# Where the split weights and the activations of a decoder layer lie in a partition

## The chip, the cores and the metric

The kernel runs on one core of a Trainium2 chip. The metric is device time of one execution in microseconds (us); lower is better. Engines are TensorE (PE, with its weight loads PEld), VectorE (DVE), ScalarE (ACT), GpSimd (POOL) and SyncE (SP).

## The reference

One inference step of one layer (D_MODEL 2048) on 256 prompt tokens and 8 x 4 sample tokens, in fp32. Cut to what matters:

```python
def hybrid_layer(x, conv_a_buf, gdn_buf, S0, w_in, ...):
    proj = x @ w_in                                   # 2048 x 11280
    gB, gC, h, q, k, v, z, b_logit, a_logit, m_a, m_b = jnp.split(proj, split_points, axis=-1)
    conv_out, new_conv_a = causal_depthwise_conv(gC * h, conv_a_buf, conv_a_w)
    y_a = (gB * conv_out) @ w_a_out
    qkv, new_gdn_buf = causal_depthwise_conv(jnp.concatenate([q, k, v], -1), gdn_buf, gdn_conv_w)
    ...                                               # gated delta rule in chunks of 64, norm, silu(z)
    y_b = o.reshape(Bsz, L, D_GDN).astype(x.dtype) @ w_b_out
    merged = jax.nn.sigmoid(m_a) * y_a + jax.nn.sigmoid(m_b) * y_b
    x = layer_norm(ALPHA * x + merged @ w_o, ln1_g, ln1_b)
    hid = jnp.square(jax.nn.relu(x @ w_up))           # 2048 x 8192
    x = layer_norm(ALPHA * x + hid @ w_down, ln2_g, ln2_b)
    return x, new_conv_a, new_gdn_buf, S.astype(S0.dtype)
```

## The kernel before

All tokens (256 + 32 = 288 columns, `NT`) stand in the free dimension; features lie on the 128 partitions, in k tiles of 128 (`KT` = 16 for 2048 features). A fp32 product is made of three fp32r matmuls: the weights are split into `hi` (rounded) and `lo` (the rest), the activations likewise, and hi x high, hi x low and lo x high are summed in PSUM.

Weights pass in blocks of 512 x 256 (four k tiles of 256 output columns; blocks of the first group and those of paired groups have `kb` = 2 k tiles of 512 columns). The list `blocks` is the order of the work, written out by hand: input projection (kqv, conv, z), gates merged with `w_a_out` and `w_b_out`, `w_o`, then four times an up-projection of 2048 columns and the down-projection that uses it. The main loop runs over the blocks. For block i it lets ACT make `his[i + 3]` from `raw[i + 3]` (`split_hi`, L187), DVE make `los[i + 3]` (`split_lo`, recorded at L142, the helper `tt`), and then issues the 24 matmuls of block i (`matmuls`, L219 for hi, L221 for lo): for each k tile, hi half 0 with the high and the low activations, hi half 1 with both, then lo half 0 and lo half 1 with the high ones. Each matmul loads its own 128 x 128 weights. The evacuation of a finished group is hung on the next blocks. The first six blocks are split just ahead of their use, with parts of a block at a time (`split_first`, and `step` in the split functions). Loads go through SP's queue, seven blocks ahead.

Buffers before: `raw`, `hi` and `lo` are tiles of 4096 bytes in a partition, four of each, in the pool `wp`; a block's k tiles follow each other at 1024 bytes (2048 where `kb` is 2). Behind `wp` stands the pool `xp` with `xh` and `xl` (later reused by the hidden activations `hh` and `hl`), 16 rows of 288 x 4 = 1152 bytes. Then come `ap` (`ao`) and, after the projection, `p3`: `R1` (`ahl`, `mh`, `acc`), `R4` (`ohl`, then `dh`), `R3` (`mg`, then `dl`), and `R2` (`ml`). `dh` and `dl` are the high and low halves of the activations of the up-projection; they have `NX` = 290 columns, of which the first up-projection uses 290 (two more for the norm's gain and bias) and the later ones 288. Start addresses in a partition, modulo 256 bytes: all of `raw`, `hi`, `lo`, `xh`, `xl`, `mh`, `ml`, `ahl`, `ohl` and `dh` 128, `dl` 0.

The last block (`by_token`, `products`, L739) has the roles turned: activations are the loaded weights, `hi` and `lo` the moving operand. The gates' small tiles (`gu`, `ge`, `gw`, `gea`, `gsb`, `s4`, `s1`) hold a few columns each in the pool `cp`.

Of the kernel before, what the change touches and what calls it, by code (L numbers as in the profile page):

```python
# [9 lines left out]
F32 = mybir.dt.float32  # L10
F32R = mybir.dt.float32r
# [5 lines left out]
P = 128  # L17
# [2 lines left out]
NS = 32  # L20
NT = NP_ + NS
NX = NT + 2
KT = D // P
H = 8
DFF = 8192
# [8 lines left out]
GW = 256  # L34
KB = 4
# [70 lines left out]
def hybrid_kernel(ctx: ExitStack, tc: tile.TileContext, A):  # L106
# [6 lines left out]
    cp = pool("cp")  # L113
    wp = pool("wp", 4)
    xp = pool("xp")
# [6 lines left out]
    def nm(s):  # L122
        counter[0] += 1
        return f"{s}{counter[0]}"
# [13 lines left out]
    act, dve, pe, gps, sp = nc.scalar, nc.vector, nc.tensor, nc.gpsimd, nc.sync  # L138


    def tt(out, a, b, op):
        dve.tensor_tensor(out=out, in0=a, in1=b, op=op)  # L142
# [14 lines left out]
            blocks.append((gi, row0 + j * kb * P, j * kb, j == 0, j == nk // kb - 1))  # L157

    raw, his, los = {}, {}, {}
    due = {}  # L160
    fill = []

# [19 lines left out]

    def split_hi(i, step=KB):
        if i < len(blocks):
            his[i] = wp.tile([P, KB, GW], F32R, tag="hi", name=nm("hi"))
            for k in range(0, KB, step):
                act.copy(his[i][:, k:k + step], raw[i][:, k:k + step])  # L187

    def split_lo(i, step=KB):
        if i < len(blocks):  # L190
            los[i] = wp.tile([P, KB, GW], F32R, tag="lo", name=nm("lo"))
            r = raw[i] if blocks[i][0].get("by_token") else raw.pop(i)
            for k in range(0, KB, step):
                tt(los[i][:, k:k + step], r[:, k:k + step], his[i][:, k:k + step], SUB)

    def matmuls(i):
        gi, r0, k0, first, last = blocks[i]
        if gi.get("by_token"):
            return first_tokens(i, k0)
        members = gi.get("pair", (gi,))  # L200
        if first:
            for m in members:
                m["ps"] = acp.tile([P, 2, 512], F32, tag="acc", name=nm("acc"))
        ps = members[0]["ps"]
        h, l = his.pop(i), los.pop(i)
        ah, al = gi["acts"]()
        n = gi["width"]
        kb = gi["kb"]
        h, l = (u.rearrange("p k c -> p (k c)").rearrange("p (k c) -> p k c", k=kb) for u in (h, l))
        for k in range(kb):  # L210
            xh_, xl_ = ah[:, k0 + k, 0:n], al[:, k0 + k, 0:n]
            st = first and k == 0
            en = last and k == kb - 1
            per = gi["cols"] // P // len(members)
            for u, m in enumerate(members):
                ts = [(m["ps"][:, t, 0:n], slice((per * u + t) * P, (per * u + t + 1) * P)) for t in range(per)]
                both = [(o, c, x) for o, c in ts for x in (xh_, xl_)]
                for o, c, x in both[::2] + both[1::2] if i == 0 else both:
                    pe.matmul(o, h[:, k, c], x, start=st and x is xh_, stop=False)  # L219
                for o, c in ts:  # L220
                    pe.matmul(o, l[:, k, c], xh_, start=False, stop=en)  # L221
                    if fill:
                        fill.pop(0)()
        if last:
            for n, f in enumerate(gi["evac"]):
                at(i + 1 + n, lambda f=f: f(ps))
# [190 lines left out]
    def wo_evac(p):  # L417
        q = slice(2 * p, 2 * p + 2)

        def resid(ps):  # L420
            pl = ph["pool"]
            if p == 0:
                ph["dl"] = pl.tile([P, KT, NX], F32R, tag="R3", name="dl")
                ph["dh"] = pl.tile([P, KT, NX], F32R, tag="R4", name="dh")
                t = ap_.tile([P, 2, H, NT], F32, tag="ao", name="lns").rearrange("p a h t -> p (a h) t")
                ph["qa"], ph["da"], ph["c"] = t[:, 0:2], t[:, 2:4], t[:, 4]
                ph["ln"] = [t[:, 5 + u] for u in range(4)]
                dh, dl = ph["dh"], ph["dl"]
                gbc = lnp[:, 0:32].rearrange("p (a k) -> p k a", a=2)
                act.copy(hmr, ones)  # L430
                act.copy(dh[:, :, NT:NX], gbc)
                tt(dl[:, :, NT:NX], gbc, dh[:, :, NT:NX], SUB)
            ph["s"] = pl.tile([P, 2, NT], F32, tag="yt", name=nm("s"), bufs=2)
            dd = ph["s"]
            stt(dd, xh[:, q, :], ALPHA, ps[:, :, 0:NT], MUL, ADD)
            stt(dd, xl[:, q, :], ALPHA, dd, MUL, ADD)
            if p:
                tt(dd, dd, bmid(ph["c"], 2), SUB)

        def centre(ps):  # L440
            tt(ph["c"], ph["s"][:, 0, :], ph["s"][:, 1, :], ADD)
            ph["chl"] = high_low(ph["c"], "sg")

        def shift(ps):
            cps = gtile()
            dd = ph["s"]
            row_sums(cps[:, 0:NT], ph["chl"])
            act.mul(ph["c"], cps[:, 0:NT], 1.0 / 256)
            tt(dd, dd, bmid(ph["c"], 2), SUB)

        def scaled(ps):
            dd, qa, da = ph["s"], ph["qa"], ph["da"]
            sd = ph["pool"].tile([P, 2, NT], F32, tag="sg", name=nm("sd"), bufs=2)
            for u in range(2):
                k = 2 * p + u
                dve.tensor_scalar(out=sd[:, u, :], in0=dd[:, u, :], scalar1=lnp[:, k:k + 1], scalar2=None, op0=MUL)
            act.copy(ph["dh"][:, q, 0:NT], sd)
            tt(ph["dl"][:, q, 0:NT], sd, ph["dh"][:, q, 0:NT], SUB)

        def sums(ps):  # L460
            dd, qa, da = ph["s"], ph["qa"], ph["da"]
            if p == 0:
                act.activation(qa, dd, AF.Square)
                act.copy(da, dd)
# [267 lines left out]
    def products(out, b, j, ks=range(KB)):  # L732
        h, l = kept[j]
        c = slice(b * P, b * P + P)
        for k in ks:
            kk = KB * j + k
            en = kk == KT - 1
            for x, w, stop in ((ph["hh"], h, False), (ph["hh"], l, False), (ph["hl"], h, en)):
                pe.matmul(out, x[:, kk, c], w[:, k, :], start=False, stop=stop)  # L739

    def first_tokens(i, k0):
        kept.append((his.pop(i), los.pop(i)))
# [273 lines left out]
    def gates(first):  # L1016
# [29 lines left out]
        be = cp.tile([P, 3, 2, 8], F32, name="be")  # L1046
        beta, g = be[:, :, 0, :], be[:, :, 1, :]
        act.activation(beta, bs[:, :, 0:8], AF.Sigmoid)
        u = cp.tile([P, 3, 8], F32, name="gu")
        e = cp.tile([P, 3, 8], F32, name="ge")  # L1050
        w = cp.tile([P, 3, 8], F32, name="gw")
        ea = cp.tile([P, 8], F32, name="gea")
        tt(u, bs[:, :, 8:16], bmid(arow[:, 1, :], 3), ADD)
        stt(e, u, -1.0, u, MUL, MIN)
        act.activation(e, e, AF.Exp)
# [11 lines left out]
        sb = cp.tile([P, 2, 8], F32, name="gsb")  # L1067
# [33 lines left out]
        s4 = cp.tile([P, 4, 8], F32, name="s4")  # L1101
        s1 = cp.tile([P, 4, 2], F32, name="s1")
# [489 lines left out]
    aux = []  # L1592
    steps = x_steps(0, 1)
    t0, o0 = steps[0]()
    his[0] = wp.tile([P, KB, GW], F32R, tag="hi", name=nm("hi"))
    los[0] = wp.tile([P, KB, GW], F32R, tag="lo", name=nm("lo"))
    t, h0, l0 = raw.pop(0), his[0], los[0]

    def split_first(k):
        for u in (2 * k, 2 * k + 1):  # L1600
            act.copy(h0[:, u], t[:, u])  # L1601
            tt(l0[:, u], t[:, u], h0[:, u], SUB)

    def turns(ts):
        for g in ts:
# [14 lines left out]
    turns(t0[0:2])  # L1620
    xs_out = x_sample(0)
    warm_up(1, 2)
    act.copy(h0[:, 0], t[:, 0])
    o0[0](dve.tensor_copy)
    xs_out()
    tt(l0[:, 0], t[:, 0], h0[:, 0], SUB)
    act.copy(h0[:, 1], t[:, 1])
    tt(l0[:, 1], t[:, 1], h0[:, 1], SUB)
# [14 lines left out]
    for i in range(len(blocks)):  # L1643
# [48 lines left out]
        if i == mark["merge"]:  # L1692
# [1 line left out]
            p3 = pool("p3")  # L1694
            ph["pool"] = p3
            r1 = p3.tile([P, KT, NT], F32R, tag="R1", name="ahl")
            r4 = p3.tile([P, KT, NX], F32R, tag="R4", name="ohl")
            ph["mg"] = p3.tile([P, KT, NX], F32, tag="R3", name="mg")[:, :, 0:NT]

            def halves(key, r, src):  # L1700
# [67 lines left out]
```

## Time and profile before

| what | value |
|---|---|
| median of 3 runs | 1658.85 us (1658.62 to 1660.47) |
| span of the profiled execution | 1656.8 us (its own time is not given apart; the median is 2.05 us above its span) |
| mean granted TensorE clock | 0.999 |
| PE busy | 1648.6 us, 13130 matmuls |
| PE weight loads busy | 1633.9 us, 13130 |
| DVE busy | 981.5 us |
| ACT busy | 786.0 us |
| DMA | 280.42 MB, mean 169 GB/s |

An engine's busy time is the union of its instructions. Matmuls overlap: the duration of one contains its way through the array, so the pace is read from the distance between starts. The columns of a group's row are line, engine, operation, output <- inputs, shapes and count, then busy time and mean duration of one in ns, then the idle time of the engine just before and what ended it.

### The profile page before, as it was taken

What the parts mean: (1) busy time and instruction counts of PE and PEld (TensorE: products, weight loads), DVE (VectorE), ACT (ScalarE), POOL (GpSimd) and SP (SyncE); (2) the same over time, 40 slices, a digit from 0 to 9 for tenths busy, and PEclk for the clock granted to TensorE, in tenths of its full rate; (3) what the DMA queues carried; (4) which work ended last, traced back from release to release, by engine and by line L of the source; (5) the groups of instructions that cost most, each with busy time, mean ns of one, the idle gap of its engine ahead of it and who ended that gap; (6) DMA issues with size and microseconds to landing.
All of it is one profiled execution on the core that took longest, in us unless ns stands there. A gap on an engine that the chain in (4) does not pass through costs nothing.

```text
span 1656.8 us, 31402 instructions
## 1 busy us (share of the span) xinstructions
PE 1648.6 (100%) x13130; PEld 1633.9 (99%) x13130; DVE 981.5 (59%) x1299; ACT 786.0 (47%) x1231; POOL 139.1 (8%) x273
## 2 busy tenths in 40 slices
PE   9999999999999999999999999999999999999998
PEld 8999999999999999999999999999999999999998
DVE  6788688767544444457776666444444444444466
ACT  6786756448533333334444455443334433344354
POOL 1142216133000000000000000000000000000011
PEclk9999999999999999999999999999999999999999
DMA  8555456545555555555565555555555555555552
GB/s 272 177 168 170 137 173 203 183 130 175 186 168 165 166 165 166 165 165 159 166 218 165 166 166 165 166 166 166 165 166 166 166 166 165 166 165 166 179 163 100
DMA packets 273237, 280.42 MB, mean 169 GB/s; under 512 B 13728, under 2 KB 267221, under 8 KB 272833
## 3 DMA queue, kind: packets, MB, share of 16 engines
q1 hardware_dynamic: 269190, 266.06, 51.5%
q0 software_dynamic: 3616, 12.02, 2.5%
q8 instruction: 103, 1.69, 0.4%
q10 hardware_dynamic: 288, 0.33, 0.1%
q14 instruction: 40, 0.32, 0.1%
HBM read 270.88 MB, written 7.48 MB: 168 GB/s over the span
## 4 chain that ended last, share of the span: by engine, by line
PE 98%; DVE 1%; ACT 1%; DMA 0%; issue 0%; SPq 0%; ACTq 0%
PE acc L219 62%; PE acc L221 31%; PE acc L739 1%; PE g L1327 0%; PE g L1499 0%; PE g L1519 0%; PE g L1522 0%; DMA raw<-in_w_in_dram 0%; PE g L1318 0%; PE g L1219 0%; PE g L1477 0%; DVE lo L142 0%; PE g L1511 0%; DVE w L145 0%; ACT hi L187 0%
## 5 line engine op out<-in xcount | busy, mean ns | idle before, releaser
L142 DVE TENSOR_TENSOR lo<-raw,hi 128x1024 fp32r<-128x1024 f32 (+1 forms) x503 | 607.3, 1211 | 576.8 <-ACT hi L187 575.0
L187 ACT CAST hi<-raw 128x1024 fp32r<-128x1024 f32 (+1 forms) x499 | 519.0, 1043 | 729.2 <-PE acc L219 659.1
L219 PE MATMUL acc<-xh,hi 128*128 128x288 f32 x1408 | 397.9, 298 | 1.0 <-ACT hi L1601 0.5
L219 PE MATMUL acc<-xl,hi 128*128 128x288 f32 x1408 | 394.2, 295 | 0.0
L221 PE MATMUL acc<-xh,lo 128*128 128x288 f32 x1408 | 302.6, 296 | 0.2 <-DVE lo L142 0.2
L219 PE MATMUL acc<-dl,hi 128*128 128x288 f32 (+1 forms) x1024 | 287.7, 295 | 0.0
L219 PE MATMUL acc<-dh,hi 128*128 128x288 f32 (+1 forms) x1024 | 287.4, 295 | 0.0
L219 PE MATMUL acc<-hl,hi 128*128 128x288 f32 x992 | 277.8, 295 | 0.0
L219 PE MATMUL acc<-hh,hi 128*128 128x288 f32 x992 | 277.4, 294 | 0.0
L219 PEld LDWEIGHTS acc<-xh,hi 128*128 128x128 f32 x1408 | 264.3, 188 | 3.8 <-issue 1.6
L219 PEld LDWEIGHTS acc<-xl,hi 128*128 128x128 f32 x1408 | 264.2, 188 | 1.0 <-DVE xl L142 0.2
L221 PEld LDWEIGHTS acc<-xh,lo 128*128 128x128 f32 x1408 | 226.0, 188 | 0.7 <-DVE lo L142 0.6
L221 PE MATMUL acc<-dh,lo 128*128 128x288 f32 (+1 forms) x1024 | 219.8, 296 | 0.0
L221 PE MATMUL acc<-hh,lo 128*128 128x288 f32 x992 | 213.2, 296 | 0.0
L219 PEld LDWEIGHTS acc<-dh,hi 128*128 128x128 f32 x1024 | 193.3, 189 | 0.0
L219 PEld LDWEIGHTS acc<-dl,hi 128*128 128x128 f32 x1024 | 192.8, 188 | 0.0
L219 PEld LDWEIGHTS acc<-hh,hi 128*128 128x128 f32 x992 | 186.4, 188 | 0.4 <-issue 0.4
L219 PEld LDWEIGHTS acc<-hl,hi 128*128 128x128 f32 x992 | 186.1, 188 | 0.0
L221 PEld LDWEIGHTS acc<-dh,lo 128*128 128x128 f32 x1024 | 164.5, 188 | 0.0
L221 PEld LDWEIGHTS acc<-hh,lo 128*128 128x128 f32 x992 | 159.0, 188 | 0.0
L219 PE MATMUL acc<-mh,hi 128*128 128x288 f32 x256 | 71.9, 297 | 0.0
L219 PE MATMUL acc<-ml,hi 128*128 128x288 f32 x256 | 71.7, 295 | 0.0
(423 smaller groups left out, 1489.3 us busy)
## 6 DMA issues: line engine op xcount, KB each, us to landing
raw<-in_w_in_dram SPq DMA_DIRECT2D x175, 512.0 KB, 3.5
raw<-in_w_up_dram SPq DMA_DIRECT2D x128, 512.0 KB, 3.6
raw<-in_w_down_dram SPq DMA_DIRECT2D x128, 512.0 KB, 3.6
raw<-in_w_o_dram SPq DMA_DIRECT2D x32, 512.0 KB, 4.0
raw<-in_w_a_out_dram SPq DMA_DIRECT2D x16, 512.0 KB, 3.6
raw<-in_w_b_out_dram SPq DMA_DIRECT2D x16, 512.0 KB, 3.6
S<-in_state_gdn_dram POOLq DMA_DIRECT2D x8, 512.0 KB, 5.7
out_dram<-S POOLq DMA_DIRECT2D x8, 512.0 KB, 4.7
```

Of the source, the lines that this page charges most:

```text
L142: dve.tensor_tensor(out=out, in0=a, in1=b, op=op)
L187: act.copy(his[i][:, k:k + step], raw[i][:, k:k + step])
L219: pe.matmul(o, h[:, k, c], x, start=st and x is xh_, stop=False)
L221: pe.matmul(o, l[:, k, c], xh_, start=False, stop=en)
L739: pe.matmul(out, x[:, kk, c], w[:, k, :], start=False, stop=stop)
```

## The change

`hi` and `lo` of a block move into one tile. There are four such tiles, made once (`wbuf`), of 4 + 2 x 1024 + 32 floats: four floats of lead, the even k tiles of hi and lo, 32 floats of gap, the odd k tiles. So odd k tiles of the weights lie 128 bytes further, modulo 256, than even ones. Behind each stands a tile of 24 floats, and ahead of `xh` one of 40 floats; they take over the gates' small tiles. `dh` and `dl` get rows of 352 columns (1408 bytes), of which 290 are used; `ohl` gets 288. All activation rows then step by 1152 or 1408 bytes, which is 128 modulo 256, and begin at the same residue, 144 bytes behind that of the weights. The instructions and their order are the same; the split functions and the matmuls address the new places.

```diff
+NXS = 352
...
+    wbuf, small = [], []
+    for u in range(4):
+        wbuf.append(wp.tile([P, 4 + 2 * 1024 + 32], F32R, tag=f"w{u}", name=f"w{u}", bufs=1))
+        small.append(wp.tile([P, 24], F32, tag=f"s{u}", name=f"small{u}", bufs=1))
+    small.append(xp.tile([P, 40], F32, tag="s4", name="small4"))
+
+    def weight_halves(i):
+        views = []
+        for o in (4, 516):
+            t = wbuf[i % 4][:, o:o + 512]
+            views.append(bass.AP(t.tensor, t.offset, [t.ap[0], (1056, 2), (256, 2), (1, 256)]))
+        return views
+
+    def by_parity(t, i):
+        return t.rearrange("p (u r) c -> p r u c" if blocks[i][0]["kb"] == KB else "p (r u) c -> p r u c", r=2)
+
+    def split_parts(i, step):
+        if step == KB:
+            return [(slice(None), slice(None))]
+        wide = blocks[i][0]["kb"] < KB
+        if step == 2:
+            return [(k, slice(None)) if wide else (slice(None), k) for k in range(2)]
+        return [(k // 2, k % 2) if wide else (k % 2, k // 2) for k in range(KB)]
...
     def split_hi(i, step=KB):
         if i < len(blocks):
-            his[i] = wp.tile([P, KB, GW], F32R, tag="hi", name=nm("hi"))
-            for k in range(0, KB, step):
-                act.copy(his[i][:, k:k + step], raw[i][:, k:k + step])
+            his[i] = weight_halves(i)[0]
+            r = by_parity(raw[i], i)
+            for a, b in split_parts(i, step):
+                act.copy(his[i][:, a, b], r[:, a, b])
...
     def split_lo(i, step=KB):
         if i < len(blocks):
-            los[i] = wp.tile([P, KB, GW], F32R, tag="lo", name=nm("lo"))
...
+            los[i] = weight_halves(i)[1]
+            r = by_parity(raw[i] if blocks[i][0].get("by_token") else raw.pop(i), i)
+            for a, b in split_parts(i, step):
+                tt(los[i][:, a, b], r[:, a, b], his[i][:, a, b], SUB)
...
-        h, l = (u.rearrange("p k c -> p (k c)").rearrange("p (k c) -> p k c", k=kb) for u in (h, l))
+        h, l = ([u[:, k % 2, k // 2] for k in range(KB)] if kb == KB else
+                [u[:, k].rearrange("p u c -> p (u c)") for k in range(2)] for u in (h, l))
...
-                    pe.matmul(o, h[:, k, c], x, start=st and x is xh_, stop=False)
+                    pe.matmul(o, h[k][:, c], x, start=st and x is xh_, stop=False)
...
-                    pe.matmul(o, l[:, k, c], xh_, start=False, stop=en)
+                    pe.matmul(o, l[k][:, c], xh_, start=False, stop=en)
...
-                ph["dl"] = pl.tile([P, KT, NX], F32R, tag="R3", name="dl")
-                ph["dh"] = pl.tile([P, KT, NX], F32R, tag="R4", name="dh")
+                ph["dl"] = pl.tile([P, KT, NXS], F32R, tag="R3", name="dl")[:, :, 0:NX]
+                ph["dh"] = pl.tile([P, KT, NXS], F32R, tag="R4", name="dh")[:, :, 0:NX]
...
-                pe.matmul(out, x[:, kk, c], w[:, k, :], start=False, stop=stop)
+                pe.matmul(out, x[:, kk, c], w[:, k % 2, k // 2], start=False, stop=stop)
...
-            r4 = p3.tile([P, KT, NX], F32R, tag="R4", name="ohl")
+            r4 = p3.tile([P, KT, NT], F32R, tag="R4", name="ohl")
```

More of the change, by code (lines that the diff above doesn't have):

```diff
@@ L184, in split_hi @@
         if i < len(blocks):
-            his[i] = wp.tile([P, KB, GW], F32R, tag="hi", name=nm("hi"))
-            for k in range(0, KB, step):
-                act.copy(his[i][:, k:k + step], raw[i][:, k:k + step])
+            his[i] = weight_halves(i)[0]
+            r = by_parity(raw[i], i)
+            for a, b in split_parts(i, step):
+                act.copy(his[i][:, a, b], r[:, a, b])
     def split_lo(i, step=KB):
         if i < len(blocks):
-            los[i] = wp.tile([P, KB, GW], F32R, tag="lo", name=nm("lo"))
-            r = raw[i] if blocks[i][0].get("by_token") else raw.pop(i)
-            for k in range(0, KB, step):
-                tt(los[i][:, k:k + step], r[:, k:k + step], his[i][:, k:k + step], SUB)
+            los[i] = weight_halves(i)[1]
+            r = by_parity(raw[i] if blocks[i][0].get("by_token") else raw.pop(i), i)
+            for a, b in split_parts(i, step):
+                tt(los[i][:, a, b], r[:, a, b], his[i][:, a, b], SUB)
     def matmuls(i):
@@ L1048, in gates @@
         act.activation(beta, bs[:, :, 0:8], AF.Sigmoid)
[L1049 to L1052, printed above, removed]
+        u, e, w = (t.rearrange("p (q h) -> p q h", h=8) for t in small[0:3])
+        ea = small[3][:, 16:24]
         tt(u, bs[:, :, 8:16], bmid(arow[:, 1, :], 3), ADD)
@@ L1066, in gates @@
         tt(gm, bmid(g[:, 2, :], 8), bc(cst("bm3"), 8), MUL)
-        sb = cp.tile([P, 2, 8], F32, name="gsb")
+        sb = small[3][:, 0:16].rearrange("p (q h) -> p q h", h=8)
         for w4 in range(4):
@@ L1100, in gates @@
         next(first)
-        s4 = cp.tile([P, 4, 8], F32, name="s4")
-        s1 = cp.tile([P, 4, 2], F32, name="s1")
+        s4 = small[4][:, 0:32].rearrange("p (q h) -> p q h", h=8)
+        s1 = small[4][:, 32:40].rearrange("p (q h) -> p q h", h=2)
         tt(s4[:, 0:2], q[:, 128:144].rearrange("p (q h) -> p q h", h=8), bmid(cst("sel"), 2), MUL)
@@ L1594, in hybrid_kernel @@
     t0, o0 = steps[0]()
-    his[0] = wp.tile([P, KB, GW], F32R, tag="hi", name=nm("hi"))
-    los[0] = wp.tile([P, KB, GW], F32R, tag="lo", name=nm("lo"))
-    t, h0, l0 = raw.pop(0), his[0], los[0]
+    his[0], los[0] = weight_halves(0)
+    t = raw.pop(0)
+    h0, l0 = ([u[:, k // 2, k % 2] for k in range(KB)] for u in (his[0], los[0]))
     def split_first(k):
         for u in (2 * k, 2 * k + 1):
-            act.copy(h0[:, u], t[:, u])
-            tt(l0[:, u], t[:, u], h0[:, u], SUB)
+            act.copy(h0[u], t[:, u])
+            tt(l0[u], t[:, u], h0[u], SUB)
     def turns(ts):
@@ L1622, in hybrid_kernel @@
     warm_up(1, 2)
-    act.copy(h0[:, 0], t[:, 0])
+    act.copy(h0[0], t[:, 0])
     o0[0](dve.tensor_copy)
     xs_out()
-    tt(l0[:, 0], t[:, 0], h0[:, 0], SUB)
-    act.copy(h0[:, 1], t[:, 1])
-    tt(l0[:, 1], t[:, 1], h0[:, 1], SUB)
+    tt(l0[0], t[:, 0], h0[0], SUB)
+    act.copy(h0[1], t[:, 1])
+    tt(l0[1], t[:, 1], h0[1], SUB)
     fill.extend([second_tile, idle, idle, idle, second_half])
```

## The prediction

> **What bounds the kernel now.** I read the page first (span, busy shares, chain of waits, costliest groups), then the matmuls stage by stage in the view of stretches of time, then single matmul starts in the timeline.
>
> ```profile
> span 1656.8 us, 31402 instructions
> PE 1648.6 (100%) x13130; PEld 1633.9 (99%) x13130; DVE 981.5 (59%) x1299; ACT 786.0 (47%) x1231; POOL 139.1 (8%) x273
> PEclk9999999999999999999999999999999999999999
> PE 98%; DVE 1%; ACT 1%; DMA 0%; issue 0%; SPq 0%; ACTq 0%
> L142 DVE TENSOR_TENSOR lo<-raw,hi 128x1024 fp32r<-128x1024 f32 (+1 forms) x503 | 607.3, 1211 | 576.8 <-ACT hi L187 575.0
> L187 ACT CAST hi<-raw 128x1024 fp32r<-128x1024 f32 (+1 forms) x499 | 519.0, 1043 | 729.2 <-PE acc L219 659.1
> L219 PE MATMUL acc<-xh,hi 128*128 128x288 f32 x1408 | 397.9, 298 | 1.0 <-ACT hi L1601 0.5
> L219 PE MATMUL acc<-dh,hi 128*128 128x288 f32 (+1 forms) x1024 | 287.4, 295 | 0.0
> ```
>
> TensorE is busy 1648.6 of 1656.8 us at the full granted clock, and 98% of the chain of waits is its own work. Its matmuls wait for nothing (idle before them 0.0 to 1.0 us); ACT's split waits for TensorE (659.1 us), not the other way. So only what shortens or lengthens one matmul moves the end, and it moves it by 11,808 matmuls of this kind (1408 x 3 with xh/xl, and likewise 1024 x 3, 992 x 3, 256 x 3, and 384 + 384 for ahl and ohl). The 298 ns "of one" is latency: matmuls overlap. The price is the distance between starts, which I take from whole stages: each stage below is 768 matmuls (8 column groups x 16 k tiles x 6).
>
> ```profile
> core 0: us, PE busy (x) PEld busy (x) DVE busy (x) ACT busy (x), PEclk, DMA share, GB/s
> ...
> 827.46:930.68 103.22, 102.86 (x771) 102.75 (x769) 6.01 (x8) 1.06 (x7) 1.00 0.58 186
> 930.68:1032.65 101.97, 101.97 (x770) 101.97 (x769) 5.97 (x8) 5.65 (x9) 1.00 0.53 166
> 1032.65:1134.89 102.24, 102.24 (x770) 102.24 (x769) 0.75 (x1) 4.53 (x7) 1.00 0.54 165
> 1134.89:1236.86 101.97, 101.97 (x771) 101.97 (x769) 5.23 (x7) 0.65 (x1) 1.00 0.53 166
> ```
>
> First row: up-projection with 290 columns (dh/dl), 103.22/768 = 134.4 ns. Second and fourth: down-projection (hh/hl), 132.77 ns, equal to the last digit. Third: up-projection with 288 columns, 133.13 ns. Nothing waits here, yet a pass over dh/dl costs 0.36 ns more than one over hh/hl with the same columns. What differs is where the operands lie.
>
> **Places.** I call "distance" the start of the activations minus the start of the weights in a partition, modulo 256 bytes. Before: all weight buffers and xh/xl (so hh/hl) begin at the same residue, weight tiles step by 1024, activations by 288 x 4 = 1152; so the distance is 0 for even k and 128 for odd k. dh and dl step by 290 x 4 = 1160 and dl begins 128 further: for tile k it is 136k for dh and 136k + 128 for dl, a new pair each tile, half of them not multiples of 16. After: 144 in every matmul; across a tile's end the next weights stand at 16. Inside one pass the timeline shows what distance does. First two k tiles of hh/hl (each six matmuls: hi with hh, hi with hl, the same for the second half of the columns, then two lo); the first column is the start in us, the second the time to the end of the last:
>
> ```profile
> 1200.21 0.29 PE L219 MATMUL acc<-hh,hi 128*128 128x288 f32 x1
> ...
> 1200.61 0.29 PE L219 MATMUL acc<-hl,hi 128*128 128x288 f32 x1
> 1200.73 0.43 PE L221 MATMUL acc<-hh,lo 128*128 128x288 f32 x2
> 1201.00 0.29 PE L219 MATMUL acc<-hh,hi 128*128 128x288 f32 x1
> ...
> 1201.40 0.30 PE L219 MATMUL acc<-hl,hi 128*128 128x288 f32 x1
> 1201.54 0.43 PE L221 MATMUL acc<-hh,lo 128*128 128x288 f32 x2
> 1201.80 0.29 PE L219 MATMUL acc<-hh,hi 128*128 128x288 f32 x1
> ```
>
> The even tile (distance 0) takes 0.79, the odd one (128) 0.80; the fourth matmul takes 0.12 in the one and 0.14 in the other. Now tiles 2, 5, 6, 7 and 14 of one column group over dh/dl, by the first start of each tile and of the next:
>
> ```profile
> 1251.23 0.29 PE L219 MATMUL acc<-dh,hi 128*128 128x288 f32 x1
> ...
> 1252.03 0.29 PE L219 MATMUL acc<-dh,hi 128*128 128x288 f32 x1
> ...
> 1253.63 0.29 PE L219 MATMUL acc<-dh,hi 128*128 128x288 f32 x1
> ...
> 1254.44 0.29 PE L219 MATMUL acc<-dh,hi 128*128 128x288 f32 x1
> ...
> 1255.22 0.29 PE L219 MATMUL acc<-dh,hi 128*128 128x288 f32 x1
> ...
> 1256.03 0.29 PE L219 MATMUL acc<-dh,hi 128*128 128x288 f32 x1
> ...
> 1260.83 0.29 PE L219 MATMUL acc<-dh,hi 128*128 128x288 f32 x1
> ...
> 1261.62 0.29 PE L219 MATMUL acc<-dh,hi 128*128 128x288 f32 x1
> ```
>
> Six equal matmuls take 0.80 in tile 2 (dh 16, dl 144), 0.81 in tile 5 (168, 40), 0.78 in tile 6 (48, 176), 0.81 in tile 7 (184, 56) and 0.79 in tile 14 (112, 240): 130.8 ns a matmul in tiles 6 and 14 (0.785/6), 135.0 in 5 and 7, whose distances are no multiples of 16. [...]
>
> **The change part by part.** *Constant distance of 144.* No row shows a long stretch at 144, so I bound it. Cheapest: every matmul at the shortest start distance, 0.12 to 0.13 above, call it 126.5 ns; dearest: as in tiles 5 and 7, 135.0. Against 132.77 for 8,736 matmuls, 133.13 for 2,304 and 134.4 for 768 these are -55 - 15 - 6 = -76 us (1583) and +19 + 4 + 0.5 = +24 us (1683). Between them, tile 2 holds both distances of the changed kernel, mixed, at about 133.3: +5 us for the 8,736, nothing for the rest. But a matmul's time follows its predecessors as well as its own distance: with distance 0 throughout, the even tile has a start 0.12 after the one before it and, over the rest, 0.13 to 0.14. In every row the distances change from tile to tile, so each tile inherits a displaced start; with one distance everywhere the row of starts can settle, and I expect it to settle near the good tiles. I take 130.8 ns: 8,736 x 1.97 = 17.2 us; 2,304 x 2.3 = 5.3 us; 768 x 2.8 (two more columns, 0.8, taken off) = 2.1 us; together 24.6 us.
> [...]
>
> *hi and lo of a block in one tile.* Four tiles hold what four hi and four lo buffers held; the split stays one ACT copy (1043 ns) and one DVE subtraction (1211 ns) a block with the same elements, in runs of 256. Cost nothing: 729.2 and 576.8 us of idle time stand before them. The thinnest cover is near 100 to 130 us of the span:
>
> ```profile
> 100.00:130.00 30.00, 29.77 (x223) 29.45 (x223) 26.75 (x49) 24.26 (x50) 3.22 (x7) 1.00 0.58 175
> ```
>
> The columns after the stretch's length are the busy time of PE, weight load, DVE, ACT and POOL. DVE is busy 26.75 of 30 us there, so faster matmuls gain nothing in about 20 us (0.3 us lost of the gain). The longest wait of ACT, with its total, count and longest case:
>
> ```profile
> ACT hi L187 <- PE acc L219: 659.1, 347, 4.0
> ```
>
> ACT writes block i + 3 into the tile that block i - 1 has just left. If it has to wait for that block's lo matmuls too, it starts two matmuls (0.27 us) later; behind it in ACT's queue stand the copies out of PSUM, and DVE's lo waits for it, but a block lasts 24 x 132.8 = 3.19 us and three blocks less 2.3 us of splitting remain: nothing for PE. SP's loads are released by the lo split as before, SP's and POOL's queues keep their order.
>
> *The rest.* Wider dh/dl rows, ohl at 288 columns and the gates' small tiles in the gaps change addresses, not instructions: nothing. The last block's 96 token-major matmuls swap roles (activations as weights); at some 120 ns they are 11.5 us, and 2% of that is 0.2 us.
>
> Sum: -24.6 + 0.3, rounded -24. The span is 1656.8 and the median of the runs 1658.85, so some 2 us lie around it. 1658.85 - 24 = 1635 us.
>
> **Rivals.** *No effect:* the whole 132.77 ns is a cost of the matmul as such, and place only shuffles the starts. For it: hh/hl passes are 101.97 each time although their single starts differ; against it: 0.78 against 0.81. Time: 1655.5 to 1662. *It settles slow (the other side):* a constant distance repeats one collision in every matmul, with no good tile to make up for it. For it: tile 2, which has these very distances, is not among the good ones. At its 133.3 ns 1664 us, at 135.0 ns 1683; it decides from a settled 133.2 ns on. *One tile for hi and lo makes PE wait:* if a matmul on hi has to wait for the whole tile, DVE's 1.2 us come before each first matmul of the six starting blocks, which are split just in time: up to 6 x 1.2 = 7 us, 1666 if the distance brought nothing. Later blocks are covered.
>
> **How the numbers follow.** 0.2% is 3.3 us, about what a measurement of this kernel can tell from none. Settles fast 0.60 (1583 to 1655, most likely 1635); no effect 0.14; settles slow 0.22; the wait 0.04. Faster 0.60, same 0.14, slower 0.26. Range: from 1590, leaving the cheapest end to less than 1 in 10, to 1672, which takes in tile 2's price and half the way to the dearest. The likeliest case's own range is 1600 to 1652.
>
> **What would show it.** Right: in the down- and up-projections 768 matmuls take about 100.5 us, both passes alike, and starts repeat every six matmuls instead of twelve. The 290-column pass differs by its columns alone. Split rows keep 1.05 and 1.2 us. Wrong: stages at 102 us (no effect), above 102.4 (settled slow), or matmuls of the first 15 us with idle time before them that ends with DVE's lo.

## The result and the profile after

| | before | after |
|---|---|---|
| median (runs) | 1659.09 us (4) | 1642.16 us (4; 1641.44 to 1643.23) |
| ratio after/before | | 0.9896, interval 0.9882 to 0.991 |
| span of the profiled execution | 1656.8 us | 1640.2 us |

16.9 us or 1.0% faster, where the prediction had 24 us. On another chip, beside the experiments, the same kernel took 1643.04 us, ratio 0.9897 (0.988 to 0.9913). The page of the changed kernel, first its span, busy shares and chain, then the groups that answer to those shown of before:

```profile
span 1640.2 us, 31402 instructions
PE 1631.2 (99%) x13130; PEld 1616.4 (99%) x13130; DVE 981.1 (60%) x1299; ACT 785.4 (48%) x1231; POOL 139.0 (8%) x273
PE 99%; DMA 0%; DVE 0%; ACT 0%; SPq 0%; issue 0%
L143 DVE TENSOR_TENSOR w<-raw,w 128x1024 fp32r<-128x1024 f32 (+1 forms) x503 | 607.3, 1210 | 561.3 <-ACT w L212 559.6
L212 ACT CAST w<-raw 128x1024 fp32r<-128x1024 f32 (+1 forms) x499 | 518.2, 1041 | 711.3 <-PE acc L245 643.2
L245 PE MATMUL acc<-xh,w 128*128 128x288 f32 x1408 | 396.4, 298 | 0.7 <-ACT w L1625 0.4
L247 PE MATMUL acc<-xh,w 128*128 128x288 f32 x1408 | 299.2, 293 | 0.5 <-DVE w L143 0.5
```

The instructions are the same in number, the splits last as long as before (1210 and 1041 ns), and PE is as full as before. PE's busy time fell by 17.4 us and the span by 16.6: every matmul got a little shorter, no wait went away. The duration of one (293 to 298 ns) shows nothing of it, because matmuls overlap: in the stages below each starts some 131 ns after the one before. Those stages show it. The view of stretches, first two of before that the prediction did not show: the 2,208 matmuls over `xh`/`xl`, `ahl` and `ohl` ahead of `w_o`, and the `w_o` pass. Then after: the same 2,208, `w_o` (`mh`/`ml`), the up-projection with 290 columns, a down-projection and an up-projection with 288 columns, 768 matmuls each:

```profile
431.90:725.22 293.32, 293.32 (x2210) 293.32 (x2209) 11.27 (x15) 10.37 (x16) 1.00 0.53 166
725.22:827.46 102.24, 102.14 (x770) 102.03 (x769) 5.98 (x8) 0.00 (x0) 1.00 0.52 164
```

```profile
core 0: us, PE busy (x) PEld busy (x) DVE busy (x) ACT busy (x), PEclk, DMA share, GB/s
429.13:718.62 289.49, 289.49 (x2210) 289.49 (x2209) 11.27 (x15) 10.34 (x16) 1.00 0.58 168
718.62:819.59 100.97, 100.87 (x770) 100.76 (x769) 5.98 (x8) 0.00 (x0) 1.00 0.55 165
819.59:923.77 104.18, 103.81 (x770) 103.70 (x769) 6.00 (x8) 1.06 (x7) 1.00 0.58 185
923.77:1024.48 100.71, 100.71 (x770) 100.71 (x769) 5.98 (x8) 5.65 (x9) 1.00 0.55 168
1024.48:1125.18 100.70, 100.70 (x771) 100.70 (x769) 0.75 (x1) 4.51 (x7) 1.00 0.54 168
```

Up and down passes with 288 columns now agree: 100.70/768 = 131.12 ns a matmul against 132.77 and 133.13. The pass with 290 columns went the other way, 103.22 to 104.18. The starts of the stages give the whole account. Up to `w_o` 6.60 us are gained (725.22 to 718.62, 4,992 matmuls), in `w_o` 1.27; the 290-column pass gives 0.96 back; then each of the first three down-projections gains 1.26 to 1.28, each of the three up-projections about 1.54 (102.24 against 100.70), and the last down-projection with all behind it 1.24. The first stretch is worth less than its matmuls would give. Its last 2,208 go from 132.84 to 131.11 ns (293.32/2,208 and 289.49/2,208), 3.83 us; the 2,784 ahead of them give 2.77, where 1.65 ns each would be 4.6.

Of these missing 1.8 us, 0.75 stand at the very start: the thirteenth matmul over `xh`/`xl` begins at 8.71 us instead of 7.96, and in the chain of waits the first weights took 5.54 us to land instead of 4.79. Whether that belongs to the change is open. The change touches neither the load nor its place in the queue; but in a second profile of the changed kernel, taken beside the experiments, this load took 4.75 us, the chain went through a load of the activations instead, and the thirteenth matmul began no earlier (8.99). The merged tile alone does not delay it, to judge by one profile: with it and the distances of before (below) that matmul began at 7.74.

### The profile page after: what moved, and what is told of

It reads as the page before. It is cut to its first block, busy times and chain, and to the rows that moved or that the text cites. A ratio compares the mean times of both kernels' runs of the same rounds, so it can differ in the third digit from the quotient of the medians.

```text
span 1640.2 us, 31402 instructions
## 1 busy us (share of the span) xinstructions
PE 1631.2 (99%) x13130; PEld 1616.4 (99%) x13130; DVE 981.1 (60%) x1299; ACT 785.4 (48%) x1231; POOL 139.0 (8%) x273
## 4 chain that ended last, share of the span: by engine, by line
PE 99%; DMA 0%; DVE 0%; ACT 0%; SPq 0%; issue 0%
PE acc L245 63%; PE acc L247 31%; PE acc L765 1%; DMA raw<-in_w_in_dram 0%; PE g L1351 0%; PE g L1523 0%; PE g L1543 0%; PE g L1546 0%; PE g L1342 0%; PE g L1243 0%; PE g L1501 0%; PE g L1535 0%; PE g L1057 0%; PE g L982 0%; PE g L719 0%; PE g L1418 0%
## 5 line engine op out<-in xcount | busy, mean ns | idle before, releaser
L143 DVE TENSOR_TENSOR w<-raw,w 128x1024 fp32r<-128x1024 f32 (+1 forms) x503 | 607.3, 1210 | 561.3 <-ACT w L212 559.6
L212 ACT CAST w<-raw 128x1024 fp32r<-128x1024 f32 (+1 forms) x499 | 518.2, 1041 | 711.3 <-PE acc L245 643.2
L245 PE MATMUL acc<-xh,w 128*128 128x288 f32 x1408 | 396.4, 298 | 0.7 <-ACT w L1625 0.4
L245 PE MATMUL acc<-xl,w 128*128 128x288 f32 x1408 | 390.8, 293 | 0.1
L247 PE MATMUL acc<-xh,w 128*128 128x288 f32 x1408 | 299.2, 293 | 0.5 <-DVE w L143 0.5
L245 PE MATMUL acc<-dh,w 128*128 128x288 f32 (+1 forms) x1024 | 287.1, 296 | 0.0
L245 PE MATMUL acc<-dl,w 128*128 128x288 f32 (+1 forms) x1024 | 285.6, 294 | 0.0
L245 PE MATMUL acc<-hh,w 128*128 128x288 f32 x992 | 276.9, 295 | 0.0
L245 PEld LDWEIGHTS acc<-xh,w 128*128 128x128 f32 x1408 | 264.4, 188 | 3.7 <-issue 1.6
L247 PEld LDWEIGHTS acc<-xh,w 128*128 128x128 f32 x1408 | 224.4, 188 | 1.0 <-DVE w L143 0.9
L247 PE MATMUL acc<-dh,w 128*128 128x288 f32 (+1 forms) x1024 | 217.3, 293 | 0.0
L247 PE MATMUL acc<-hh,w 128*128 128x288 f32 x992 | 209.6, 292 | 0.0
L245 PEld LDWEIGHTS acc<-dh,w 128*128 128x128 f32 x1024 | 192.4, 188 | 0.0
L245 PEld LDWEIGHTS acc<-hh,w 128*128 128x128 f32 x992 | 186.4, 188 | 0.4 <-issue 0.4
L247 PEld LDWEIGHTS acc<-dh,w 128*128 128x128 f32 x1024 | 163.4, 188 | 0.0
L247 PEld LDWEIGHTS acc<-hh,w 128*128 128x128 f32 x992 | 157.7, 188 | 0.0
```

The source lines that it names most:

```text
L212: act.copy(his[i][:, a, b], r[:, a, b])
L245: pe.matmul(o, h[k][:, c], x, start=st and x is xh_, stop=False)
L247: pe.matmul(o, l[k][:, c], xh_, start=False, stop=en)
```

## The experiments

All of them say "distance" as the prediction does. Times are set against runs of the kernel before on the same chip.

**The rows alone.** Before, with only the tidy rows of `dh`, `dl` and `ohl`:

```diff
-                ph["dl"] = pl.tile([P, KT, NX], F32R, tag="R3", name="dl")
+                ph["dl"] = pl.tile([P, KT, NXS], F32R, tag="R3", name="dl")[:, :, 0:NX]   # NXS = 352; dh likewise
-            r4 = p3.tile([P, KT, NX], F32R, tag="R4", name="ohl")
+            r4 = p3.tile([P, KT, NT], F32R, tag="R4", name="ohl")
```

> The kernel before with one part of the change alone: rows of dh and dl of 352 columns (and ohl of 288), so that dh and dl also lie at distances 0 and 128 in turn, as hh and hl do; weights untouched. Theory A (the distance between activations and weights sets the pace, and the gain comes from holding it constant at a good value): the later up-projections fall from 102.24 us per 768 matmuls to the 101.97 of the down-projections, the other stages stay, in all about -1 us, 1658. Theory B (the gain comes from tidy rows, starts at multiples of 16 bytes): a good part of the 17 us is here, 1645 to 1655.

1659.17 us against 1660.14, ratio 0.9997 (0.9987 to 1.0006). The view of stretches, for the pass with 290 columns, the first down-projection and the next up-projection:

```profile
827.88:931.66 103.78, 103.41 (x770) 103.30 (x769) 6.00 (x8) 1.06 (x7) 1.00 0.59 185
931.66:1033.63 101.97, 101.97 (x771) 101.97 (x770) 5.97 (x8) 5.64 (x9) 1.00 0.54 166
1033.63:1135.60 101.97, 101.97 (x771) 101.97 (x769) 0.75 (x1) 4.53 (x7) 1.00 0.54 166
```

The up-projection with 288 columns comes down to exactly the down-projection's 101.97, so what made the two differ before was indeed where `dh` and `dl` lie; the 290-column pass pays 0.56 us for it. Tidy rows that keep distances 0 and 128 are worth nothing measurable. Before, half of the tiles of `dh` and `dl` started at 8 modulo 16, here all start at multiples of 16. The pass of the third row got cheaper (133.13 to 132.77 ns), that of the first row dearer (103.22 to 103.78 us), so these runs do not settle whether a start at a multiple of 16 is worth anything by itself.

**Distances 16 and 144 instead of 144 alone.** The changed kernel without the 128 bytes between even and odd k tiles:

```diff
-            views.append(bass.AP(t.tensor, t.offset, [t.ap[0], (1056, 2), (256, 2), (1, 256)]))
+            views.append(bass.AP(t.tensor, t.offset, [t.ap[0], (1024, 2), (256, 2), (1, 256)]))
```

> The changed kernel without the 128 bytes by which odd tiles of the contraction lie further: the distance is 144 in even k tiles and 16 in odd ones. Theory A in its strict form (a constant distance settles the starts): the gain goes, 132 to 133 ns a matmul, 1652 to 1662 us. Rival C (16 and 144 are both good values, constancy is not needed): as the changed kernel or better, 131 ns, about 1640. Rival D (the gain comes from one tile for hi and lo, not from the distance): 1642.

1648.25 us, ratio 0.9931 (0.9916 to 0.9945): two thirds of the gain stay. A down-projection of it in the view of stretches, then the 2,208 matmuls ahead of `w_o`:

```profile
928.09:1029.02 100.93, 100.93 (x770) 100.93 (x769) 5.97 (x8) 5.64 (x9) 1.00 0.55 167
430.57:722.52 291.95, 291.95 (x2211) 291.95 (x2210) 11.26 (x15) 10.35 (x16) 1.00 0.57 166
```

The down-projection takes 131.4 ns, 0.3 from the changed kernel and 1.4 from before, and the up-projections with 288 columns the same. There a distance that is the same in every matmul is not what matters most; which distances occur does. The early stretch is another matter: 291.95/2,208 = 132.2 ns at the same two distances, 1.1 from the changed kernel. Of the 5.6 us of span that this version lacks, 3.9 are lost ahead of `w_o`. None of the three cases of the expectation came out whole.

**A constant distance of 0.** The changed kernel with the weights moved to the residue of the activations: the small tile goes in front of the weights, and the four floats of lead fall away.

```diff
+    small4 = wp.tile([P, 40], F32, tag="s4", name="small4", bufs=1)
...
-    small.append(xp.tile([P, 40], F32, tag="s4", name="small4"))
+    small.append(small4)
...
-        for o in (4, 516):
+        for o in (0, 512):
```

> The changed kernel with a constant distance of 0 instead of 144 (the tile of 40 floats ahead of the weights instead of behind, no lead of four floats). Theory A with a value that matters: another pace than 131.1 ns, by the even tiles of the kernel before 131.8 ns, 1648 us, and not the 1642 of the changed kernel. Rival E (any constant distance will do): 131.1 ns, 1642. Rival D (one tile for hi and lo): 1642.

1654.37 us, ratio 0.9969 (0.9958 to 0.9981). In the view of stretches 2,208 matmuls over `xh`, `xl`, `ahl` and `ohl`, and a down-projection over `hh` and `hl`:

```profile
431.45:722.17 290.72, 290.72 (x2211) 290.72 (x2210) 11.27 (x15) 10.36 (x16) 1.00 0.57 167
928.43:1030.41 101.98, 101.98 (x770) 101.98 (x769) 5.98 (x8) 5.64 (x9) 1.00 0.54 166
```

Constancy without the good distance leaves a third of the gain, and nearly all of it lies in the early part: 290.72/2,208 = 131.67 ns there, 132.79 later. The expectation had 1648 us from 131.8 ns throughout, so it was right for the early part alone. `xh`/`xl` and `hh`/`hl` are the same bytes, read block by block by the same code. So one geometry can run at two paces, for hundreds of matmuls each. What chooses between them the run does not show.

**Everything but the distance.** The same kernel, also without the 128 bytes, so that one tile for hi and lo, the split by parity and the wide rows stay, with distances 0 and 128 as before (shown against the changed kernel; the small tile goes in front as above):

```diff
-        for o in (4, 516):
+        for o in (0, 512):
...
-            views.append(bass.AP(t.tensor, t.offset, [t.ap[0], (1056, 2), (256, 2), (1, 256)]))
+            views.append(bass.AP(t.tensor, t.offset, [t.ap[0], (1024, 2), (256, 2), (1, 256)]))
```

> The changed kernel with the distances of the kernel before: weights without the shift of odd tiles and without lead, the 40 floats ahead of them, so 0 and 128 in turn everywhere; one tile for hi and lo, the split by parity and rows of 352 stay. Theory A: the pace is that of the kernel before, 132.77 ns, 1658 us. Rival D (part of the gain comes from one tile for hi and lo): faster than 1655.

1659.86 us, ratio 0.9998 (0.9988 to 1.0008), and its first down-projection is back at the old price:

```profile
931.66:1033.63 101.97, 101.97 (x770) 101.97 (x769) 5.98 (x8) 5.65 (x9) 1.00 0.54 165
```

The whole gain is where the operands lie. The merged tile neither costs nor brings anything. Beside the distance, the changed kernel also has its weights at an odd multiple of 16 bytes (112 modulo 128), where this version and the kernel before have them at a multiple of 32; the separate stages below take the two apart.

**The distance by itself.** A kernel with nothing of the model: stages of 192 matmuls in the kernel's pattern of six, over operands copied once, with distance, columns and row steps set by hand (`odd` is the shift of the odd k tiles, `row` the step of the activations):

```python
at = dist // 4 + row * (4 * (b % 4) + k)                  # activations, in floats
o = (k % 2) * (1024 + odd // 4) + (k // 2) * 256          # weights: hi here, lo 512 further
```

> All of the model is left out; only its stream of matmuls is run, on weights and activations copied from w_in: per stage 192 matmuls, 8 blocks of 24 in the kernel's order. 16 stages with 288 columns at constant distances 0, 16, ... 240 (tiles ca to cp); 16 with 290 columns and rows of 352 at the same distances (na to np); 16 with 288 columns and weights without the shift of odd tiles, so that the distance is d and d + 128 in turn (za to zp); four at distance 144 with 292, 296, 304 and 320 columns (sa to sd). Theory A: the pace differs by distance by 2% or more in ns a matmul, 144 is among the lowest of the first 16 at 131.1, and za (0 and 128) is 132.8 as in the kernel before. Theory E: the first 16 stages agree within 0.3%. For 290 columns theory A expects another order of the distances, since at 144 the changed kernel's pass has 135.0 ns; if two columns cost only their 0.8 ns, 131.9.

In the view of stretches, a stage from its start to the next one's: constant distances 16, 32, 112 and 144 with 288 columns, 144 and 208 with 290 columns, and last the alternating pairs 0/128 and 48/176.

```profile
core 0: us, PE busy (x) PEld busy (x) DVE busy (x) ACT busy (x) POOL busy (x), PEclk, DMA share, GB/s
45.02:70.30 25.28, 25.28 (x195) 25.28 (x193) 3.16 (x2) 5.05 (x1) 0.00 (x0) 1.00 0.01 1
70.30:96.01 25.71, 25.71 (x195) 25.71 (x194) 3.17 (x2) 5.04 (x1) 0.00 (x0) 1.00 0.00 1
197.34:223.00 25.66, 25.66 (x194) 25.66 (x193) 3.16 (x2) 5.04 (x1) 0.00 (x0) 1.00 0.01 1
248.50:273.77 25.27, 25.27 (x194) 25.27 (x193) 3.15 (x2) 5.05 (x1) 0.00 (x0) 1.00 0.01 1
658.52:684.22 25.70, 25.70 (x194) 25.70 (x193) 3.16 (x2) 5.04 (x1) 0.00 (x0) 1.00 0.01 1
762.16:788.70 26.54, 26.54 (x195) 26.54 (x193) 3.17 (x2) 5.04 (x1) 0.00 (x0) 1.00 0.00 1
840.23:865.72 25.49, 25.49 (x195) 25.49 (x193) 3.15 (x2) 5.04 (x1) 0.00 (x0) 1.00 0.00 1
916.58:941.80 25.22, 25.22 (x195) 25.22 (x194) 3.17 (x2) 5.04 (x1) 0.00 (x0) 1.00 0.00 1
```

With the full clock, next to no DMA, and on the other engines only the copies of the next stage's operands (3.16 us on DVE, 5.05 on ACT), 192 equal matmuls take 25.28 us at 16, 25.71 at 32 and 25.27 at 144. That is 1.7% between the distances, a little less than was expected, and 131.6 ns at 144 where the kernel has 131.1. The pair of the kernel before, 0/128, takes 25.49/192 = 132.8 ns, its price in the kernel. 144 is among the best constant distances, but not alone: 48/176 in turn is as good. With 290 columns the span between distances is larger (132.8 ns at 112, 138.2 at 208), and 144 takes 133.9, less than in the kernel; the third of these kernels comes back to that. The six rows with 288 columns differ in their places alone, and in time by up to 2% (25.22 to 25.71 us).

**Is it the distance or the place, and does the past count?** The same kernel with distance 144 and both operands shifted together, distance 0 likewise, stages that begin after four matmuls of other widths, and rows of 320 floats.

```python
at = (dist + shift) // 4 + row * (4 * (b % 4) + k)
o = shift // 4 + (k % 2) * (1024 + odd // 4) + (k // 2) * 256
if kick:                                                  # ahead of the stage
    for u in range(4): pe.matmul(g[:, 0, 0:kick], wbuf[u][:, 0:P], lo[:, 0:kick], start=True, stop=True)
```

> All of the model is left out; only streams of matmuls as in the first scan, 192 per stage. 16 stages at distance 144 with weights and activations together 0, 16, ... 240 bytes further (ca to cp); 8 at distance 0 with both 0, 32, ... 224 further (oa to oh); 8 equal ones at distance 144, both 112 further, each behind four matmuls of another width, 256 to 340 columns (ka to kh); 16 with activation rows of 320 columns and weights without the shift of odd tiles, distance 0 to 240 (ra to rp). [...] Rival F (the place as such, not the difference, matters): the c stages differ among themselves and all k stages agree. [...]

Distance 144 at shifts 16 and 32; distance 0 at shifts 0 and 64; a stage after another width; rows of 320 at distances 112 and 144:

```profile
44.58:69.74 25.16, 25.16 (x194) 25.16 (x193) 3.15 (x2) 5.03 (x1) 0.00 (x0) 1.00 0.00 1
69.74:95.02 25.28, 25.28 (x194) 25.28 (x193) 3.17 (x2) 5.04 (x1) 0.00 (x0) 1.00 0.00 1
422.88:448.17 25.29, 25.29 (x194) 25.29 (x193) 3.16 (x2) 5.04 (x1) 0.00 (x0) 1.00 0.00 1
473.45:498.95 25.50, 25.50 (x195) 25.50 (x194) 3.17 (x2) 5.04 (x1) 0.00 (x0) 1.00 0.00 1
626.89:652.07 25.18, 25.18 (x194) 25.18 (x193) 2.68 (x2) 4.84 (x1) 0.00 (x0) 1.00 0.00 1
1009.62:1035.47 25.85, 25.85 (x194) 25.85 (x193) 3.16 (x2) 5.05 (x1) 0.00 (x0) 1.00 0.00 1
1061.08:1086.04 24.96, 24.96 (x195) 24.96 (x193) 3.15 (x2) 5.03 (x1) 0.00 (x0) 1.00 0.00 1
```

At distance 144 all eight odd multiples of 16 give 25.16 (131.1 ns) and the multiples of 32 give 25.28 (131.65), wherever in the 256 bytes (the run's first stage, at shift 0, takes 26.95 and has this pace in its second half); at distance 0 the six shifts from 64 on give 25.50 (132.8) and the first two 25.29. So neither the activations' place nor the weights' alone decides: the same place of either is cheap at 144 and dear at 0. Their relation does, and at 144 beside it the place modulo 32: of the 1.65 ns that the changed kernel gains with 288 columns, these stages put some 0.55 to it and 1.1 to the distance. At distance 0 neither explains the two paces, since all eight shifts are multiples of 32; whether the place in the 256 bytes or what ran before makes them is open. All eight stages that began after other widths came to 131.1 to 131.3 ns, so at this distance what ran just before does not matter, as rival F had it for these stages. Rows of 320 gave the lowest pace of all, 24.96/192 = 130.0 ns at 144, but 25.85/192 = 134.6 at 112.

**Why the 290-column pass got dearer, and whether 130.0 ns can be had.** The same with the weights 112 bytes further, at the kernel's own residue modulo 128. (Modulo 256 even and odd tiles have changed places: 240 and 112 in these stages, 112 and 240 in the kernel.)

```diff
-        ps = stage("r" + LET[d], 16 * d, 288, 320, 0)
+        ps = stage("r" + LET[d], 16 * d, 288, 320, 0, 112)
+    for j, (n, row, odd) in enumerate(((288, 288, 128), (290, 352, 128), (292, 352, 128), ...)):
+        ps = stage("v" + LET[j], 144, n, row, odd, 112)
+    for d in range(8):
+        ps = stage("p" + LET[d], 144, 288, 320, 0, 16 * d)
```

> All of the model is left out; only streams of matmuls as in the scans before, 192 per stage, weights at the residue that they have in the changed kernel (112 modulo 256) unless told. 16 stages with rows of 320 columns (1280 bytes) and weights without the shift of odd tiles at distances 0 to 240, 288 columns (ra to rp) and 290 columns (ta to tp); eight at distance 144: 288 columns in rows of 288 with the shift (va), 290 and 292 in rows of 352 with the shift (vb, vc), 292, 296, 304, 320 and 256 in rows of 320 without it (vd to vh); and eight with rows of 320 at distance 144 with both operands 0 to 112 bytes further than residue 0 (pa to ph). Theory F2 (beside the distance, where the weights stand modulo 32 decides): va 131.1, vb 135.0 and vc about 134 as in the kernels, pa, pc, pe, pg agree with each other and pb, pd, pf, ph with each other, at least 0.5 ns apart. Theory A alone (the distance): all p stages 130.0.

The changed kernel's geometry with 288, 290 and 292 columns; rows of 320 at distance 144 on a multiple of 32 and 16 beside it:

```profile
836.60:861.80 25.20, 25.20 (x195) 25.20 (x194) 3.16 (x2) 5.05 (x1) 0.00 (x0) 1.00 0.01 1
861.80:887.70 25.90, 25.90 (x194) 25.90 (x193) 3.16 (x2) 5.04 (x1) 0.00 (x0) 1.00 0.00 1
887.70:913.40 25.70, 25.70 (x194) 25.70 (x193) 3.16 (x2) 5.04 (x1) 0.00 (x0) 1.00 0.01 1
1043.72:1068.69 24.97, 24.97 (x195) 24.97 (x194) 3.19 (x2) 5.04 (x1) 0.00 (x0) 1.00 0.01 1
1068.69:1094.06 25.37, 25.37 (x194) 25.37 (x193) 3.16 (x2) 5.04 (x1) 0.00 (x0) 1.00 0.00 1
```

131.2 ns with 288 columns and 134.9 with 290 (25.90/192), close to the passes in the kernel (131.12; 135.2 when the 0.37 us in which PE idles are taken off the 104.18). So the dearer pass needs no cause outside these operands: at this geometry two more columns cost 3.7 ns, and two more again take 1.0 off. In the first of these kernels, with the weights at a multiple of 32, 290 columns at 144 took 133.9. Rows of 320 depend on the weights' place still more: at distance 112 they took 134.6 ns above and take 130.0 here, where only both operands stand 112 bytes further.

**292 columns in the kernel.** The changed kernel with `NX = NT + 4`, the gain and bias twice:

```diff
-NX = NT + 2
+NX = NT + 4
```

> The changed kernel with 292 columns in the first up-projection instead of 290 (the pair of columns for gain and bias stands twice). Theory A (a settled cycle of collisions sets the pace, and the number of columns is part of it as the distance is): by the stage of 292 columns at distance 144 in the scan, 132.8 ns instead of 135.0, 768 matmuls 1.7 us less, 1640.5 us. Rival (columns cost what they are wide): 0.8 ns more, 1642.8 us.

```profile
819.70:923.06 103.36, 102.99 (x770) 102.88 (x769) 6.01 (x8) 1.06 (x7) 1.00 0.59 187
```

The pass with more work takes 0.82 us less than the changed kernel's 104.18, as the third kernel of separate stages says in sign and size (0.20 us in 192, 0.8 in 768); the 1.7 us expected came from the first, whose weights stand elsewhere. In the whole it cannot be told: 1641.56 us, ratio 0.989 (0.9875 to 0.9905).

**The best geometry of the separate stages in the kernel.** `mh`, `ml`, `dh` and `dl` with rows of 320, their weights without the shift of odd tiles, distance 112; the other activations are moved along with the pool:

```diff
-NXS = 352
+NXS = 320
...
-            views.append(bass.AP(t.tensor, t.offset, [t.ap[0], (1056, 2), (256, 2), (1, 256)]))
+            views.append(bass.AP(t.tensor, t.offset, [t.ap[0], (1024 if blocks[i][0].get("flat") else 1056, 2), (256, 2), (1, 256)]))
...
+            p3.tile([P, 56], F32, tag="lead", name="lead")
```

> A version that may beat both: the changed kernel, with w_o and the up-projections at the best place of the scans: mh, ml, dh, dl in rows of 320 columns, weights of these blocks without the shift of odd tiles, constant distance 112 with the weights at 112 modulo 256; all other stages stay at 144. Theory F2 (distance, residue modulo 32, row and columns fix the pace, whatever else runs): by the scan's stages 130.0 ns in w_o and the up-projections with 288 columns (3072 matmuls, -3.4 us) and 134.9 with 290 columns (as in the changed kernel), 1638.7 us. Rival (the streams of the scan, with no other engine at work, do not carry over): 1642 or more.

The changed kernel ran beside it:

> The changed kernel once more, for the comparison on the same chip: 1642 us by all theories.

1643.28 us (ratio 0.9901, 0.9886 to 0.9915) beside 1643.04 for the changed kernel: nothing is gained. A stretch of the separate stages (distance 112, rows of 320), then the up-projection with 288 columns in the kernel:

```profile
196.88:221.84 24.96, 24.96 (x194) 24.96 (x193) 3.16 (x2) 5.05 (x1) 0.00 (x0) 1.00 0.01 1
```

```profile
1025.09:1125.79 100.70, 100.70 (x770) 100.70 (x769) 0.75 (x1) 4.52 (x7) 1.00 0.55 168
```

130.0 ns alone, 131.12 in the kernel, at the same distance. The geometry is not quite the same: the separate stage has its weights at 240 modulo 256 and the kernel at 112. Besides, in the kernel loads and splits run beside the matmuls (the DMA share is 0.55 there and 0.01 in the separate stage) and the groups follow in another rhythm; which of these keeps it at 131.12 was not tried and stays open. No version beat the changed kernel by more than the measurement can tell.

## Why the prediction was right, and where it was not

*Direction right, cause right in kind, the value 144 partly luck.* PE's pace was the whole bound, and it hung on where the operands lie. Putting the distances alone back to those of before takes the gain to nothing (ratio 0.9998); the tidy rows alone bring nothing (0.9997). The reading that carried the prediction was 0.78 against 0.81 us for six equal matmuls in one pass. The step from there to this change, that with one distance everywhere the row of starts settles near the good tiles, is no rule: at a constant 0 the passes from `w_o` on stayed at 132.8 ns, constant distances of 32 and 112 took more than the kernel before in the first separate stages, and 16 and 144 in turn kept two thirds of the gain. The single tiles were a poor guide to a distance too. With two distances in turn from tile to tile (in tile 2 and tile 14 they stood inside one tile), separate stages took 131.6 ns at 16 and 144, the pair of tile 2, which counted as not good, and 133.2 at 112 and 240, the pair of tile 14, which counted as good. No row of before pointed to 144, and that it is among the good distances was luck as far as the prediction goes.

*The settled pace: mis-sized.* The prediction took 130.8 ns from two single tiles. The 288-column stages measured 131.12, the long early stretch 131.11. Two tiles read in hundredths of a microsecond could not tell 130.8 from 131.1, and over 11,040 matmuls that third of a nanosecond is 3.5 us. By the starts of the stages the 17.2 us for the 8,736 matmuls became 12.9 (6.60 up to `w_o`, 1.27 in `w_o`, 5.05 in the down-projections and the end), and the 5.3 us for the 2,304 became 4.6 (3 x 1.54). This term, the next one and the early stretch make up the miss, 16.6 us of span against 24.3.

*The 290-column pass: wrong in sign.* The prediction had it 2.1 us cheaper, with the two columns at 0.4 ns each. That was their price before: with PE's idle time taken off, its two passes over `dh`/`dl` take 102.86 us with 290 columns and 102.24 with 288, 0.81 ns a matmul apart. The pass got 0.96 us dearer. The separate stages put the two columns at 3.7 ns in this geometry, and the 292-column kernel showed that the price does not even rise with the columns (103.36 us against 104.18). The step that failed is "the 290-column pass differs by its columns alone".

*Lost in the thin cover: right in size, but not all that was lost.* From 96.8 us on, 216 matmuls take 29.71 us where they took 29.74, so the 0.36 us that the new pace would bring there is missing, as the prediction had it (0.3). The first 2,784 matmuls together fall short by 1.8 us, though. 0.75 of it is the later start, and the remaining 0.7 is spread over the first 430 us, where other matmuls stand between these, and was not followed further.

*Starts that repeat every six: not so.* The timeline of the changed kernel over `hh` and `hl`, two k tiles and the beginning of a third (start, time to the end of the last):

```profile
1190.47 0.30 PE L245 MATMUL acc<-hh,w 128*128 128x288 f32 x1
1190.60 0.30 PE L245 MATMUL acc<-hl,w 128*128 128x288 f32 x1
1190.73 0.29 PE L245 MATMUL acc<-hh,w 128*128 128x288 f32 x1
1190.87 0.29 PE L245 MATMUL acc<-hl,w 128*128 128x288 f32 x1
1190.99 0.42 PE L247 MATMUL acc<-hh,w 128*128 128x288 f32 x2
1191.26 0.29 PE L245 MATMUL acc<-hh,w 128*128 128x288 f32 x1
1191.39 0.29 PE L245 MATMUL acc<-hl,w 128*128 128x288 f32 x1
1191.52 0.29 PE L245 MATMUL acc<-hh,w 128*128 128x288 f32 x1
1191.65 0.29 PE L245 MATMUL acc<-hl,w 128*128 128x288 f32 x1
1191.78 0.42 PE L247 MATMUL acc<-hh,w 128*128 128x288 f32 x2
1192.04 0.30 PE L245 MATMUL acc<-hh,w 128*128 128x288 f32 x1
```

The two tiles take 0.79 and 0.78, with steps that differ, although their distances do not. The row of starts has settled, but into a pattern of two tiles. Over whole passes it still repeats every twelve matmuls, as before.

*The rivals.* "No effect" fell with 100.70 us a pass. "It settles slow" did not come about at 144, but it is a real case of the same kind: constant distances of 32 and 112 take 133.9 and 133.7 ns in the first separate stages, above its deciding point of 133.2. The prediction could not tell 144 from 32 by a rule. "One tile makes PE wait" fell: PE's idle time before L247 is 0.5 us in all.

## What to carry to other kernels

When PE is full and its matmuls wait for nothing, look at the distance between starts by stage: passes with the same shapes and different paces (here 101.97 and 102.24 us) point to where the operands lie, and moving them cost no instruction (31402 before and after). Measure a few relative places of weights and activations on the chip in a small kernel of the same pattern before choosing, then confirm in the kernel, because the best place of the small kernel need not be the best there (here 130.0 ns alone and 131.12 in the kernel). Single tiles read from the trace of a mixed row, in hundredths of a microsecond, are too coarse to choose by. Odd widths such as 290 columns deserve a stage of their own: the next larger width can be cheaper (here 103.36 us with 292 against 104.18).

## What the runs showed of the hardware

- The place of the moving operand relative to the weights, told modulo 256 bytes, changed the pace of 128x128x288 fp32r matmuls, each with its own weight load, by 1.7% with rows of 288 floats (131.65 ns at 16, 133.9 at 32). At one distance the place modulo 32 bytes counted too: 131.1 against 131.65 ns at 144 with rows of 288 floats, and with rows of 320 floats 130.0 against 132.1 at 144 and 134.6 against 130.0 at 112.
- Some paces came back in quite different kernels and stages: 131.1 ns (the changed kernel; separate stages at 144 on odd multiples of 16), 131.65 (separate stages at 16, and at 144 on multiples of 32; 131.67 early in the kernel at a constant 0) and 132.8 (the kernel before; separate stages at 0/128, and at 0 from shift 64 on).
- One geometry kept two paces in one kernel: 131.67 and 132.79 ns at distance 0, 132.2 and 131.4 at 16 and 144 in turn. What chooses between them no run showed.
- The separate stages with 288 columns differ in their places alone, and in time by up to 2% (25.22 to 25.71 us). Why one place costs more than another, by a collision or otherwise, no run showed.
